# A hybrid encoder layer on one core: another way to the recurrence's decay, another order of the split products, and pools that wait by bytes

## The chip, the cores and the metric

The kernel runs on one core of one Trainium2 chip. The metric is the device time of one execution in microseconds (us), from the profiler's clock, as the median of several runs. The core has TensorE (PE, the matrix engine, with its weight loads listed as PEld), VectorE (DVE), ScalarE (ACT), GpSimd (POOL), and SyncE (SP), whose queue issues most of the DMA transfers.

## The reference, cut to what matters

One layer of a streaming encoder for 1,024 prompt tokens and 32 sample tokens, with 1,024 channels:

```python
z = x @ w_in + b_in                      # 12 sections of 1024 columns
# mixer A: short gated convolution; mixer C: HGRN2, a matrix state in 8 heads
# mixer B: a per-channel linear recurrence on the convolved section xf
r  = sigmoid(xf . w_a + b_a);  gi = sigmoid(xf . w_x + b_x)
log_a = -8 * r * softplus(-lam)
a  = exp(log_a)
u  = sqrt(-expm1(2 * log_a)) * (gi * xf)
h_t = a_t * h_{t-1} + u_t                # over the tokens
yB = (gelu(gB) * h) @ w_out_b
m  = sigmoid(gA)*yA + sigmoid(gB)*yB + sigmoid(gC)*yC
x  = LayerNorm(alpha*x + m @ w_o)
x  = LayerNorm(alpha*x + PEER(x))        # 8 heads x top 16 of 16,384 single-neuron experts
```

## The kernel before, in words

Channels lie on the 128 partitions and tokens along the free axis. The tokens go in two halves: half 0 is 512 prompt tokens, half 1 is the other 512 and the 32 sample tokens with a gap (548 columns, two segments of 274).

**Split products.** Every projection of the layer that decides which experts are chosen is done in three products: weight and activation are each split in a high and a low part. `weight` (line 286) loads a raw slice of 1024 x 128, casts it to `wh` on ScalarE (L292), and subtracts on VectorE to get `wl` (L293). Two buffers each of raw, `wh` and `wl` go round. `proj` (line 319) then walks over the 8 slices k of the contraction: `wh` times the activations' high part (L326), `wh` times their low part (L327), and `wl` times the high part (L329), for each of one or two segments, into PSUM tiles named `z`.

**Mixer B.** `mix_b` (line 555) does one tile of 128 channels: it is called 8 times for each half. After the gates' matmul (L585), ScalarE computes `tr` and `ti` (tanh forms of the two sigmoids, L589 and L591), `t` (L592, a tanh of half of -log_a) and `sq` (L593, the square root of t). VectorE computes 1/(1+t) (L599 or, in half 1, ScalarE's L597, then L600), a = 1 - 2t/(1+t) (L601, then L605 or, in half 1, ScalarE's L603), the input of the recurrence (L607 to L609), and the scan (L615).

**Stages and pools.** The SBUF is a stack of pools that stages open and close through `open` (line 118). A stage's pool often lies where an earlier stage's pool lay. Half 0's retrieval of experts (`topk`, `retrieve`) works in the pool `rp`, 12 buffers of 2,240 bytes a partition. It closes, and half 1's HGRN2 heads open `hp` (15,872 bytes) from the same start and `xe` (6 buffers of 2,208 bytes) behind it. `head_c` (line 627) evacuates its projection z of the query into an `xe` tile through ScalarE (L637), after two other `xe` tiles are made (L647, L648).

**Half 0's experts** are gathered token by token: GpSimd issues an indirect DMA for each of 1,024 rows of a table (L1210; four row buffers), and VectorE uses each row (L1219 for the table u, L1227 for v). These VectorE instructions are placed among the other VectorE work by counts of PE instructions (`pacing`). **Half 1's experts** are computed densely: `dense` (line 1103) walks over 16 chunks of 8 x 128 experts. In each, 8 hidden slices are projected (those of the first chunks are computed earlier), weighted (L1123) and split in `dh` and `dl` (L1127, L1128), and then 8 projections take these 8 pairs as their slices k.

**Order.** The program is traced in order, and a list scheduler with a timing model places each engine's instructions by priority and by when it thinks they are ready, so that an engine's order may differ from the trace's. On the chip, each engine then runs its list strictly in that order.

Of the kernel before, what the change touches and what calls it, by code (L numbers as in the profile page):

```python
# [16 lines left out]
AF = mybir.ActivationFunctionType  # L17
OP = mybir.AluOpType
# [4 lines left out]
KT = 8  # L23
# [48 lines left out]
FA = 2  # L72
# [29 lines left out]
class K:  # L102
# [15 lines left out]
    def open(self, ctx, **pools):  # L118

        for name, (bufs, kw) in pools.items():  # L120
            setattr(self, name, ctx.enter_context(self.tc.tile_pool(name=name, bufs=bufs, **kw)))

    def et(self, n=556, dt=F32):
        return self.ep.tile([128, n], dt, name="e", tag="e")
# [28 lines left out]
    def consts(self):  # L153
        nc, io, c = self.nc, self.io, self.cst
        V, A, G = nc.vector, nc.scalar, nc.gpsimd
# [28 lines left out]
        ct = ExitStack()  # L184
        t = ct.enter_context(self.tc.tile_pool(name="ct", bufs=1))
# [47 lines left out]
        e8 = lambda nm: c.tile([128, 8], F32, name=nm)  # L233
# [35 lines left out]
        self.sp2 = e8("sp2")  # L269
        V.tensor_scalar(u, u, 2.0, None, op0=OP.mult)  # L270
        V.scalar_tensor_tensor(self.sp2, p, 4.0, u, op0=OP.mult, op1=OP.add)


        self.ha = c.tile([128, 8, 2], F32, name="ha")
# [44 lines left out]
    def proj(self, w, x, lay):  # L319
        mm = self.nc.tensor.matmul  # L320
        z = self.zz(lay)
        wh, wl = w
        for k in range(KT):
            xh, xl = x[k]
            for (o, n), ps in zip(lay.segs, z):
                mm(ps[:, :n], wh[:, k, :], xh[:, o:o + n], start=k == 0, stop=False)  # L326
                mm(ps[:, :n], wh[:, k, :], xl[:, o:o + n], start=False, stop=False)  # L327
            for (o, n), ps in zip(lay.segs, z):
                mm(ps[:, :n], wl[:, k, :], xh[:, o:o + n], start=False, stop=k == KT - 1)  # L329
        return z  # L330
# [224 lines left out]
    def mix_b(self, ct, out):  # L555
        nc, par, b, L = self.nc, self.par, self.b, self.L
        V, A, mm, N = nc.vector, nc.scalar, nc.tensor.matmul, L.N
        col = lambda p: par[:, p + ct:p + ct + 1]
        zx = self.proj(self.win(B_X, ct), self.x, L)
        u = self.et()  # L560
        V.tensor_copy(u[:, 0:3], self.hbx[:, ct, :])
        for v, p in L.each(zx):
            A.activation(v(u, 3), p, AF.Identity, bias=col(B_X * 8))
        if b:
            V.tensor_copy(u[:, SO:SO + 3], par[:, P_SCB + 3 * ct:P_SCB + 3 * ct + 3])
            V.tensor_copy(self.st[:, 32 + 3 * ct:35 + 3 * ct], u[:, HB:HB + 3])
            V.tensor_copy(self.st[:, 56 + 3 * ct:59 + 3 * ct], u[:, SO + SMP:SO + SMP + 3])
        else:
            V.tensor_copy(self.hbx[:, ct, :], u[:, HB:HB + 3])
        cb = self.et()  # L570
        A.activation(cb[:, :N], u[:, 0:N], AF.Identity, scale=col(P_CBW), bias=col(P_CBB))
        for k in (1, 2, 3):
            V.scalar_tensor_tensor(cb[:, :N], u[:, k:k + N], col(P_CBW + 8 * k), cb[:, :N],
                                   op0=OP.mult, op1=OP.add)
        zg = self.proj(self.win(B_G, ct), self.x, L)
        g = self.et()
        for v, p in L.each(zg):
            A.activation(v(g), p, AF.Gelu, bias=col(B_G * 8))
        yield
        pr, pi = (self.zz(L), self.zz(L)) if b else ([self.tt()], [self.tt()])  # L580
        lw = self.lp.tile([128, 2, 128], F32, name="lw", tag="lw")
        nc.sync.dma_start(lw, self.io["lru_w"][ct])
        for j, z in enumerate((pr, pi)):
            for v, p in L.each(z):
                mm(p, lw[:, j, :], v(cb), start=True, stop=True)  # L585
        tr, ti, sq = self.et(), self.et(), self.et()
        t = tr
        for v, p in L.each(pr):
            A.activation(v(tr), p, AF.Tanh, scale=0.5, bias=self.hlb[:, ct:ct + 1])  # L589
        for v, p in L.each(pi):  # L590
            A.activation(v(ti), p, AF.Tanh, scale=0.5, bias=self.hlb[:, 8 + ct:9 + ct])  # L591
        A.activation(t[:, :N], tr[:, :N], AF.Tanh, scale=self.sp2[:, ct:ct + 1], bias=self.sp2[:, ct:ct + 1])  # L592
        A.activation(sq[:, :N], t[:, :N], AF.Sqrt)  # L593

        rc, a = self.et(), t
        if b and FA > 1:
            A.activation(rc[:, :N], t[:, :N], AF.Identity, bias=self.one)  # L597
        else:
            V.tensor_scalar(rc[:, :N], t[:, :N], 1.0, None, op0=OP.add)  # L599
        V.reciprocal(rc[:, :N], rc[:, :N])  # L600
        V.tensor_mul(a[:, :N], t[:, :N], rc[:, :N])  # L601
        if b and FA:
            A.activation(a[:, :N], a[:, :N], AF.Identity, scale=-2.0, bias=self.one)  # L603
        else:
            V.tensor_scalar(a[:, :N], a[:, :N], -2.0, 1.0, op0=OP.mult, op1=OP.add)  # L605
        v = ti
        V.scalar_tensor_tensor(v[:, :N], ti[:, :N], 1.0, cb[:, :N], op0=OP.add, op1=OP.mult)  # L607
        V.tensor_mul(v[:, :N], v[:, :N], sq[:, :N])
        V.tensor_mul(v[:, :N], v[:, :N], rc[:, :N])  # L609
        if b:  # L610

            V.memset(a[:, SO - 1:SO], 0.0)
            V.tensor_copy(v[:, SO - 1:SO], col(P_SLR))
        h = cb
        V.tensor_tensor_scan(h[:, :N], a[:, :N], v[:, :N], self.hl[:, ct:ct + 1],  # L615
                             op0=OP.mult, op1=OP.add)
        if b:
            V.tensor_copy(self.st[:, 80 + ct:81 + ct], h[:, HB - 1:HB])
            V.tensor_copy(self.st[:, 88 + ct:89 + ct], h[:, SO + SMP - 1:SO + SMP])
        else:  # L620
            V.tensor_copy(self.hl[:, ct:ct + 1], h[:, HB - 1:HB])
        r = self.yraw(True)
        V.tensor_mul(r[:, :N], g[:, :N], h[:, :N])
        out.append(self.yfin(r))
# [770 lines left out]
```

## Time and profile before

| | |
|---|---|
| median of 3 runs | 4206.25 us (4188.08 to 4211.31) |
| profiled execution, its own time | 4205.61 us |
| its span, first to last instruction | 4203.8 us |
| PE busy | 3815.1 us (91%), 26,917 matmuls |
| PE weight loads busy | 3564.2 us (85%) |
| VectorE busy | 3389.8 us (81%) |
| ScalarE busy | 1461.2 us (35%) |
| GpSimd busy | 1591.6 us (38%) |
| granted TensorE clock, mean | 0.952 of full speed |

The span and the profiled execution's own time differ by 1.8 us. Stages follow each other: up to about 740 us half 0's mixers, to about 1235 us half 0's norm and retrieval beside half 1's mixer A, to about 1670 us half 1's heads, to about 1970 us half 1's mixer B, to about 2340 us norm and retrieval, to about 2732 us the choice of experts spread to a dense form, and from there the dense experts. The gathers run from 988 us to the end.

### The profile page before, as it was taken

The page shows a single profiled execution, that of the slowest core. Times are in us where ns is not written, and L with a number is a line of the kernel's source. Part 1 is how long each engine was busy: PE and PEld are TensorE (multiplying, and loading weights), DVE is VectorE, ACT ScalarE, POOL GpSimd, SP SyncE. Part 2 cuts the span into 40 slices and gives each one's busy share as a digit, 9 for nine tenths or more (in the row PEclk, how much of TensorE's full clock was granted, in tenths as well). Part 3 has the DMA queues.
Part 4 walks back from the last instruction along what each step waited for, and adds up shares of the span by engine and source line. Part 5 has one row for each costly group of instructions (what it writes and reads, how often), then busy time and mean ns, then how long its engine had stood idle before and what let it go on. Part 6 is the DMA issues. An engine that isn't in the chain of part 4 may idle for free.

```text
span 4203.8 us, 69644 instructions
## 1 busy us (share of the span) xinstructions
PE 3815.1 (91%) x26917; PEld 3564.2 (85%) x26917; DVE 3389.8 (81%) x6793; ACT 1461.2 (35%) x2358; POOL 1591.6 (38%) x1353
## 2 busy tenths in 40 slices
PE   9999999998866998998878999789999999999997
PEld 7888777787765896998868999689999999999997
DVE  6565448589997787998899999967788878777888
ACT  3333337332212222454233389822222222222222
POOL 0000000002453344444552478823355555455553
PEclk9999999999887998999989999899999999999998
DMA  3222222345785666778986888698889988888886
GB/s 109 76 71 78 90 92 92 129 154 195 255 284 183 197 226 194 249 271 279 316 287 206 266 247 245 202 325 302 283 315 325 324 303 312 299 313 302 311 313 243
DMA packets 333451, 973.51 MB, mean 232 GB/s; under 512 B 29952, under 2 KB 104832, under 8 KB 331072
## 3 DMA queue, kind: packets, MB, share of 16 engines
q0 software_dynamic: 147456, 536.94, 37.6%
q1 hardware_dynamic: 185664, 432.12, 30.3%
q8 instruction: 212, 3.47, 0.3%
q14 instruction: 119, 0.97, 0.1%
HBM read 912.40 MB, written 56.54 MB: 230 GB/s over the span
## 4 chain that ended last, share of the span: by engine, by line
PE 50%; DVE 15%; issue 14%; DMA 10%; POOL 9%; ACT 2%; POOLq 0%; SPq 0%; DVEq 0%; ACTq 0%
PE z L329 14%; PE z L326 14%; PE z L327 14%; POOL row L1210 9%; DMA row<-in_v,ex 6%; DVE row L1219 2%; DVE wl L293 2%; DVE x1g L1227 2%; DMA row<-in_u,ex 2%; PE t L1073 2%; PE t L681 1%; PE z L336 1%; DVE oa L1069 1%; DVE e L960 1%; DVE e L959 1%
## 5 line engine op out<-in xcount | busy, mean ns | idle before, releaser
L326 PE MATMUL z<-h,wh 128*128 128x272 f32 (+5 forms) x4608 | 1381.8, 313 | 104.6 <-ACT xe L637 59.8
L327 PE MATMUL z<-l,wh 128*128 128x272 f32 (+5 forms) x4608 | 1377.5, 311 | 6.0 <-DVE l L908 4.8
L292 ACT CAST wh<-wraw 128x1024 fp32r<-128x1024 f32 x568 | 595.5, 1049 | 1850.5 <-PE z L327 1538.4
L1210 POOL DMA_INDIRECT row<-in_u,ex x512 | 669.0, 1307 | 1432.6 <-DVE ex L1033 667.5
L329 PE MATMUL z<-h,wl 128*128 128x272 f32 (+5 forms) x4608 | 1172.7, 312 | 10.2 <-DVE wl L293 10.1
L326 PEld LDWEIGHTS z<-h,wh 128*128 128x128 f32 x4608 | 883.0, 192 | 152.0 <-ACT xe L637 60.1
L1210 POOL DMA_INDIRECT row<-in_v,ex x512 | 682.9, 1334 | 797.5 <-DVE x1g L1227 532.2
L327 PEld LDWEIGHTS z<-l,wh 128*128 128x128 f32 x4608 | 883.4, 192 | 42.3 <-DVE l L908 5.9
L293 DVE TENSOR_TENSOR wl<-wraw,wh 128x1024 fp32r<-128x1024 f32 x568 | 692.4, 1220 | 232.5 <-ACT wh L292 231.2
L329 PEld LDWEIGHTS z<-h,wl 128*128 128x128 f32 x4608 | 778.3, 191 | 50.0 <-DVE wl L293 14.0
L1227 DVE SCALAR_TENSOR_TENSOR x1g<-row,hh,x1g 128x1024 f32<-128x1024 f32 x512 | 655.3, 1280 | 105.1 <-DMA row<-in_v,ex 101.6
L1219 DVE SCALAR_TENSOR_TENSOR row<-row,x1g 128x1024 f32<-128x1024 f32 x512 | 619.3, 1221 | 98.8 <-DMA row<-in_u,ex 98.0
L326 PE MATMUL z<-dh,wh 128*128 128x272 f32 x2048 | 556.2, 293 | 9.3 <-ACT ge L1084 4.9
L327 PE MATMUL z<-dl,wh 128*128 128x272 f32 x2048 | 558.2, 294 | 1.1 <-DVE dl L1128 1.1
L329 PE MATMUL z<-dh,wl 128*128 128x272 f32 x2048 | 436.0, 295 | 74.6 <-DVE wl L293 74.4
L326 PEld LDWEIGHTS z<-dh,wh 128*128 128x128 f32 x2048 | 391.5, 194 | 12.3 <-ACT ge L1084 5.2
L329 PEld LDWEIGHTS z<-dh,wl 128*128 128x128 f32 x2048 | 331.2, 194 | 79.4 <-DVE wl L293 79.4
L327 PEld LDWEIGHTS z<-dl,wh 128*128 128x128 f32 x2048 | 391.7, 193 | 1.7 <-DVE dl L1128 1.5
L1072 POOL TENSOR_SCALAR ob<-iota,tr 128x128 f32<-128x128 f32 x272 | 218.6, 818 | 29.4 <-PE t L1073 13.0
L329 PE MATMUL z<-yh,wl 128*128 128x512 f32 (+1 forms) x512 | 179.4, 353 | 22.5 <-DVE wl L293 22.4
L1127 ACT CAST dh<-w 128x544 fp32r<-128x544 f32 x128 | 82.5, 648 | 335.8 <-DVE w L1123 335.4
L1073 PE MATMUL t<-ob,oa 128*128 128x128 f32 x1088 | 172.8, 295 | 25.1 <-DVE oa L1069 8.5
(382 smaller groups left out, 4828.3 us busy)
## 6 DMA issues: line engine op xcount, KB each, us to landing
wraw<-in_w_in SPq DMA_DIRECT2D x192, 512.0 KB, 3.5
wraw<-in_vt SPq DMA_DIRECT2D x128, 512.0 KB, 6.4
wraw<-in_ut SPq DMA_DIRECT2D x128, 512.0 KB, 5.6
gd<-stg SPq DMA_DIRECT2D x34, 1024.0 KB, 6.1
gt<-gd SPq DMA_DIRECT2D x16, 2176.0 KB, 10.7
wraw<-in_wq SPq DMA_DIRECT2D x56, 512.0 KB, 4.3
wraw<-in_w_o SPq DMA_DIRECT2D x24, 512.0 KB, 4.9
hd<-ge SPq DMA_DIRECT2D x40, 272.0 KB, 4.8
```

What stands on the lines that cost most here:

```text
L292: nc.scalar.copy(wh, raw)
L293: nc.vector.tensor_sub(wl, raw, wh.bitcast(F32))
L326: mm(ps[:, :n], wh[:, k, :], xh[:, o:o + n], start=k == 0, stop=False)
L327: mm(ps[:, :n], wh[:, k, :], xl[:, o:o + n], start=False, stop=False)
L329: mm(ps[:, :n], wl[:, k, :], xh[:, o:o + n], start=False, stop=k == KT - 1)
L336: self.nc.tensor.matmul(ps[:, :n], w[:, k, :], x[k][:, o:o + n], start=k == 0, stop=k == KT - 1)
L1072: G.tensor_scalar(ob, self.iota, tr[:, 1, t:t + 1], None, op0=OP.is_equal)
L1073: nc.tensor.matmul(pw[:, s * 128:(s + 1) * 128], oa, ob, start=True, stop=True)
L1127: A.copy(hi, w)
L1210: nc.gpsimd.indirect_dma_start(out=u[:n], out_offset=None, in_=self.io[tab], in_offset=bass.IndirectOffsetOnAxis(ap=ex[:n, s:s + 1], axis=0))
L1219: V.scalar_tensor_tensor(u[:n], u[:n], 1.0, x1[:n], op0=OP.mult, op1=OP.mult, accum_out=hh[:n, s:s + 1])
L1227: V.scalar_tensor_tensor(x1[:n], u[:n], hh[:n, s:s + 1], x1[:n], op0=OP.mult, op1=OP.add)
```

## The change

It has three parts. In mixer B, `a` becomes an exponential on ScalarE with scale and bias `sp4` = -2 `sp2`; the reciprocal and the steps around it go; the recurrence's input becomes 0.5 (ti+1) cb (a+1) sq, which is the same quantity since 1/(1+t) = (1+a)/2. In `proj`, all products of the `wl` slices come behind all products of the `wh` slices. In `open`, each pool asks for waits by tile (`reuse_waits="tile"`): a tile waits for the earlier tiles whose bytes it takes, and no longer a whole pool for the whole of the earlier pools under it.

```diff
@@ def open
-            setattr(self, name, ctx.enter_context(self.tc.tile_pool(name=name, bufs=bufs, **kw)))
+            setattr(self, name, ctx.enter_context(self.tc.tile_pool(
+                name=name, bufs=bufs, reuse_waits="tile", **kw)))
@@ def consts
+        self.sp4 = e8("sp4")
+        V.tensor_scalar(self.sp4, self.sp2, -2.0, None, op0=OP.mult)
@@ def proj
                 mm(ps[:, :n], wh[:, k, :], xh[:, o:o + n], start=k == 0, stop=False)
                 mm(ps[:, :n], wh[:, k, :], xl[:, o:o + n], start=False, stop=False)
+        for k in range(KT):
+            xh, _ = x[k]
             for (o, n), ps in zip(lay.segs, z):
                 mm(ps[:, :n], wl[:, k, :], xh[:, o:o + n], start=False, stop=k == KT - 1)
@@ def mix_b
-        t = tr
+        t, a = sq, tr
...
         A.activation(t[:, :N], tr[:, :N], AF.Tanh, scale=self.sp2[:, ct:ct + 1], bias=self.sp2[:, ct:ct + 1])
+        A.activation(a[:, :N], tr[:, :N], AF.Exp, scale=self.sp4[:, ct:ct + 1], bias=self.sp4[:, ct:ct + 1])
         A.activation(sq[:, :N], t[:, :N], AF.Sqrt)
 
-        rc, a = self.et(), t
-        if b and FA > 1:
-            A.activation(rc[:, :N], t[:, :N], AF.Identity, bias=self.one)
-        else:
-            V.tensor_scalar(rc[:, :N], t[:, :N], 1.0, None, op0=OP.add)
-        V.reciprocal(rc[:, :N], rc[:, :N])
-        V.tensor_mul(a[:, :N], t[:, :N], rc[:, :N])
-        if b and FA:
-            A.activation(a[:, :N], a[:, :N], AF.Identity, scale=-2.0, bias=self.one)
-        else:
-            V.tensor_scalar(a[:, :N], a[:, :N], -2.0, 1.0, op0=OP.mult, op1=OP.add)
         v = ti
         V.scalar_tensor_tensor(v[:, :N], ti[:, :N], 1.0, cb[:, :N], op0=OP.add, op1=OP.mult)
-        V.tensor_mul(v[:, :N], v[:, :N], sq[:, :N])
-        V.tensor_mul(v[:, :N], v[:, :N], rc[:, :N])
+        V.scalar_tensor_tensor(sq[:, :N], a[:, :N], 1.0, sq[:, :N], op0=OP.add, op1=OP.mult)
+        V.scalar_tensor_tensor(v[:, :N], v[:, :N], 0.5, sq[:, :N], op0=OP.mult, op1=OP.mult)
```

## Rows read from the trace of the kernel before

**Rows 1.** Waits of all engines: who waited for whom, total us, times, longest

```profile
PE z L329 <- DVE wl L293: 113.7, 47, 11.0
...
PE z L326 <- ACT xe L637: 59.8, 2, 59.5
...
PE z L326 <- ACT wh L292: 46.0, 42, 9.2
```

**Rows 2.** Windows: length, busy us (count) by engine, clock, DMA share, GB/s

```profile
605.00:745.00 140.00, 140.00 (x578) 108.38 (x577) 113.65 (x141) 94.81 (x114) 0.00 (x0) 1.00 0.27 89
841.00:1261.00 420.00, 338.78 (x2497) 326.36 (x2496) 396.81 (x1304) 110.98 (x191) 133.36 (x105) 0.93 0.66 222
1727.00:1970.00 243.00, 223.76 (x1636) 218.31 (x1636) 228.44 (x343) 121.98 (x181) 108.83 (x80) 0.96 0.79 269
2732.00:4204.00 1472.00, 1357.68 (x10561) 1348.44 (x10559) 1182.54 (x1590) 374.58 (x552) 698.78 (x523) 0.96 0.86 305
3153.00:3363.00 210.00, 206.09 (x1640) 205.22 (x1639) 180.48 (x208) 56.84 (x88) 120.32 (x88) 1.00 0.91 325
```

**Rows 3.** Waits of PE alone from 2732 us to the end

```profile
PE z L329 <- DVE wl L293: 76.1, 22, 9.2
```

**Rows 4.** Timeline of PE: first and last of eight long waits in the dense stage

```profile
2834.29 0.82 PE L329 MATMUL z<-dh,wl 128*128 128x272 f32 x2 [9.13 <-DVE wl L293]
...
4038.37 0.52 PE L329 MATMUL z<-dh,wl 128*128 128x272 f32 x2 [3.87 <-DVE wl L293]
```

**Rows 5.** Timeline around 3510 us: PE, then VectorE

```profile
3514.26 0.82 PE L329 MATMUL z<-dh,wl 128*128 128x272 f32 x2 [6.47 <-DVE wl L293]
...
3511.40 1.28 DVE L1227 SCALAR_TENSOR_TENSOR x1g<-row,hh,x1g 128x1024 f32<-128x1024 f32 x1 [7.01 <-DMA row<-in_v,ex]
```

**Rows 6.** Window of 4 us behind that wait

```profile
3513.00:3517.00 4.00, 2.73 (x12) 2.74 (x13) 4.00 (x7) 0.00 (x0) 0.89 (x1) 0.50 0.74 243
```

**Rows 7.** Timeline from 1235 to 1296 us: PE, then ScalarE, then VectorE

```profile
1235.52 0.30 PE L329 MATMUL z<-h,wl 128*128 128x292 f32 x1
1295.36 0.58 PE L326 MATMUL z<-h,wh 128*128 128x256 f32 x1 [59.55 <-ACT xe L637]
...
1291.95 0.84 ACT L647 ACTIVATE xe<-e,f,f 128x544 f32<-128x544 f32 x1 [33.46 <-DVE ex L1033]
...
1291.56 0.29 DVE L1033 SCALAR_TENSOR_TENSOR ex<-r 128x128 int32<-128x128 f32 x1
```

**Rows 8.** Waits of SP's DMA queue

```profile
SPq L749 <- DVE ex L1033: 50.2, 1, 50.2
```

**Rows 9.** Mixer B by source line: count, then ns min/median/max

```profile
L592 ACT ACTIVATE e<-e,sp x16: 816/836/875, 619.7 to 1923.2; 128x512 f32<-128x512 f32 x8, 128x548 f32<-128x548 f32 x8
...
L593 ACT ACT_TABLE_LOAD  x16: 1283/1283/1283, 620.5 to 1927.6; - x16
...
L597 ACT ACTIVATE e<-e,one x8: 737/739/750, 1748.1 to 1931.3; 128x548 f32<-128x548 f32 x8
...
L599 DVE TENSOR_SCALAR e<-e x8: 420/427/428, 620.6 to 738.3; 128x512 f32<-128x512 f32 x8
...
L600 DVE RECIPROCAL e<-e x16: 3346/3440/3578, 621.0 to 1937.4; 128x512 f32<-128x512 f32 x8, 128x548 f32<-128x548 f32 x8
...
L601 DVE TENSOR_TENSOR e<-e x16: 679/700/730, 626.0 to 1948.6; 128x512 f32<-128x512 f32 x8, 128x548 f32<-128x548 f32 x8
```

**Rows 10.** Timeline, two chunk starts: first PE product, the last `dl` on VectorE

```profile
3809.79 0.29 PE L326 MATMUL z<-dh,wh 128*128 128x272 f32 x1
...
3820.82 0.72 DVE L1128 TENSOR_TENSOR dl<-w,dh 128x544 fp32r<-128x544 f32 x1
...
4021.78 0.29 PE L326 MATMUL z<-dh,wh 128*128 128x272 f32 x1
...
4025.84 0.72 DVE L1128 TENSOR_TENSOR dl<-w,dh 128x544 fp32r<-128x544 f32 x1
```

## The prediction

> **What bounds the kernel now.** I read the page first, then the waits, then windows by stage, and the timeline at the longest waits. PE is busy 3815.1 of 4203.8 us, so some 389 us of its idle time, and what the clock loses behind idle time, are all that a change which leaves the count of matmuls alone can win. The waits name the idle time [rows 1]: 113.7 us in 47 waits for the low weight part `wl`, one wait of 59.5 us for ScalarE's evacuation into an `xe` tile, and 46.0 us for the high part `wh`. By stage [rows 2] PE is full in half 0's mixer B (140.00 of 140.00 us), VectorE is nearly full from 841 to 1261 us (396.81 of 420), and the dense stage runs PE 1357.68 of 1472 us, with the DMA engines at 0.86. The window from 3153 us shows that stage undisturbed: 1640 matmuls in 210 us at full clock, 0.128 us each, DMA share 0.91.
>
> **The order of the products.** A projection of two segments is 48 matmuls. PE now meets `wl` after 4 of them; afterwards after 32, so `wl` may be 28 x 0.128 = 3.6 us later. (For one segment it is 14 matmuls, 1.8 us.) Nothing else is added: 48 products and as many weight loads stay. In the dense stage the 22 waits for `wl` sum to 76.1 us [rows 3]. Eight were longer than 3.6 us, from 9.13 down to 3.87 [rows 4], 52.1 us together; these keep 52.1 - 8 x 3.6 = 23.3 us, and the rest vanish, so 52.8 us would go. What makes `wl` late stays, though: at 3511 us VectorE stood 7.01 us at a gathered row and the subtraction was queued behind it [rows 5], and a faster PE asks for its weights sooner from DMA engines that have 0.86 to 0.91 of their time used. I take 45 us (bounds 25 and 53).
>
> The clock adds to this. After the 6.47 us wait it was granted 0.50, and PE did 12 matmuls in 2.73 busy us [rows 6] where 21 fit at 0.128: 9 x 0.128 = 1.2 us lost. Of the 16 dense waits of 1.8 us and more, the eight up to 3.6 us should end wholly: 8 x 1.2 = 10 us.
>
> The other 25 waits are 113.7 - 76.1 = 37.6 us. Most lie where VectorE leaves only 420 - 397 = 23 us [rows 2], and a wait taken off PE there partly comes back as a wait for VectorE's results. I take half, 18 us (bounds 5 and 30). `wh` is released after 32 matmuls of 48 instead of 46, 1.8 us earlier, so ScalarE can cast the next but one sooner; of the 46.0 us for `wh` most follow a late transfer, and I take 5 us (0 to 20).
>
> Against this, the last activations are needed earlier. A dense chunk's first projection starts while the eighth pair `dh`, `dl` is still being made. PE fills the time: it does 7 slices of the first projection and then 7 of the second, whose weights are the only others resident. That was 2 x 42 x 0.128 = 10.8 us of filler; afterwards the first pass of both gives 2 x 28 x 0.128 = 7.2 us, since their `wl` products stand behind the missing slice. The eighth `dl` came from 4.8 us (4021.78 to 4026.56) to 11.7 us (3809.79 to 3821.54) after the first product [rows 10]; in the eleven chunks from the sixth on, seven were later than 7.2 us, by 14 us together. Cost: 14 us (bounds 0 and 62, the second without any filler, below).
>
> **Pools that wait by bytes.** PE stopped at 1235.8 us with its PSUM tiles full, two of its projections waiting to be evacuated into `xe` tiles. ScalarE's first write to `xe` came at 1291.95, 0.1 us after VectorE's last instruction of half 0's retrieval (1291.56, 0.29 us long), and PE went on at 1295.36 [rows 7]: the whole pool waited for the whole pool. SP's queue stood 50.2 us at the same release, with the weights behind it [rows 8]. By bytes, `xe` begins 15,872 bytes into the old pool of 26,880 and ends at 29,120. Only its last buffer lies clear of retrieval tiles; the other five still wait for whichever tile of the last retrieval lies under them, the `hp` tiles do too, and ScalarE takes its list in order. So the gain lies between 0 and 59.5 us. I take a quarter, 15 us, nearer to nothing because one buffer in six is clear. The other stage changes show no wait of this kind that I can price; I take nothing for them.
>
> **The decay.** Each half-0 call drops on VectorE two scalar steps of 0.42, the reciprocal 3.44 and a product 0.70 us, 5.0 us; each half-1 call drops 3.44 + 0.70 = 4.1 us [rows 9]. Two products of the input become two of another form, taken as equal. Eight calls of each make VectorE 40 and 33 us lighter. ScalarE gains an exponential like L592 (0.84 us) and, if it needs a table of its own between the tanh's and the square root's, one more load of 1.28 us: 2.1 us a call, less 2 x 0.74 us for L597 and L603 in half 1. In half 0 all of it is hidden: PE is busy 140.00 of 140.00 us, and ScalarE goes from 94.81 to 112 us [rows 2]; without that cover it would be 8 x 2.1 = 17 us. In half 1 PE idles 243 - 223.76 = 19 us; most of that is for weights, counted above, and I take 3 us (-17 to 10).
>
> The Trainium skill (ScalarE: Activation LUTs, Table sets: the hidden batching unit) speaks against this part: it has the exponential and the square root in different sets, so that one behind the other means a load each. The trace has the load at 1.28 us; the page's own budget of about 2.66 us for a switch would make it an estimated 16 x (2.66 + 0.84) = 56 us of ScalarE's time in place of 34. By the same page tanh lies in the exponential's set too, so some loads may fall to a neighbour. No row here shows an exponential between the two.
>
> **The sum.** 45 + 10 + 18 + 5 + 15 + 3 - 14 = 82 us. From the profiled execution's 4205.61 us that gives 4124 us. Its own time is 0.6 us under the median of the runs, 4206.25, so nothing is corrected for that. The runs shown spread by 0.5%, about what a measurement of this kernel can tell from no change, 21 us.
>
> **The rivals.**
>
> *The long wait goes whole.* If the scheduler places the query's evacuation early and gives it a clear buffer, 59.5 us go instead of 15: 4124 - 45 = 4079 us. For it speaks that two evacuations free four of six PSUM tiles; against it the bytes and SP's queue.
>
> *The waits for `wl` only move.* VectorE's lateness comes from gathered rows, and those from DMA engines at 0.86 and more [rows 2, 5]. If the DMA sets the pace, PE's waits return elsewhere, and of the dense 55 us and the other 18 us a quarter and a half stay: 4124 + 41 + 9 = 4174 us. Against it speaks the window from 3153 us, with full clock at 0.91.
>
> *The table loads reach the path.* If the square root's result, late by 2.1 us in each of 16 calls, holds up PE, the time is 4124 + 34 = 4158 us. Against it speaks that VectorE's chain in the same call gets over 4 us shorter.
>
> *Slower: PE waits for the last `dl`.* If the scheduler finds no filler, PE stops 3.7 us after the first product (29 x 0.128) until the eighth `dl`, which comes at 8.1 us at the median: 4.4 us and 1.2 us of clock in each of eleven chunks, 62 us. This is then the same lateness under another name, so the dense 55 us don't come either: 4205.6 - (18 + 5 + 15 + 3) + 62 = 4227 us. It decides from 41 / 11 = 3.7 us a chunk on. Against it: PE's lists already hold such filler.
>
> **How the numbers follow.** The forecast has a chance of 0.50, with a range of its own from 4085 to 4165 us (its bounds taken together by halves). The whole wait has 0.17, the moved waits 0.17, the table loads 0.08, the slower case 0.08. From 4045 (the whole wait with the terms at their upper bounds) to 4195 us (the moved waits with some chunk waits) about 0.8 is held. Faster than 4185 are the forecast and the whole wait, most of the tables' case and three quarters of the moved one less a little for terms that all fall short: 0.82. Slower than 4227 is half of the last rival and what I can't see: 0.06. Within: 0.12.
>
> **What the profile afterwards would show.** Right: PE's waits for `wl` near 50 us in all, in the dense stage some ten in place of 22; mean clock above 0.952; no reciprocal in mixer B and VectorE's total about 73 us lower; 16 loads more on ScalarE at most; PE going on after 1235 us some 15 us earlier. Wrong: long PE waits for `dl` at chunk starts; waits for `wl` as many and as long as before; a new wait at an exponential; or the 59.5 us wait unchanged or gone.

## The result and the profile after

The changed kernel takes 4139.89 us (median of 4 runs, 4132.19 to 4149.73), the kernel before beside it on the same chip 4202.66 (4 runs). The ratio is 0.9855 [0.982, 0.9891]: faster by 62.8 us, where 82 were forecast. The profiled execution took 4132.19 us with a span of 4130.4, 73.4 us shorter than that of before; it is the shortest of the four runs, and the landmarks below are its own.

The busy time per engine on the page of the changed kernel:

```profile
PE 3792.2 (92%) x26917; PEld 3553.3 (86%) x26917; DVE 3320.1 (80%) x6746; ACT 1490.5 (36%) x2367; POOL 1578.8 (38%) x1353
```

The count of matmuls is unchanged; VectorE is 69.7 us lighter (3389.8 before). The mean granted clock rose from 0.952 to 0.958. TensorE's waits over the whole span (total us, times, longest), to be held against [rows 1]:

```profile
PE z L329 <- ACT xe L632: 60.1, 1, 60.1
PE z L329 <- ACT wh L295: 39.4, 16, 6.0
PE z L334 <- DVE wl L296: 36.3, 18, 4.1
```

The waits for `wl` fell from 113.7 to 36.3 us, those for `wh` by 6.6, and the one long wait for `xe` is as long as it was. From 2700 us to the end, against [rows 3]:

```profile
PE z L334 <- DVE wl L296: 25.3, 8, 4.1
PE z L330 <- DVE dl L1123: 18.6, 16, 2.7
PE z L329 <- ACT dh L1122: 7.4, 12, 1.2
```

Here the waits for `wl` lost 50.8 us. But `dl` and `dh`, for which TensorE had waited 2.4 us in this stage, now cost 26.0 us: nearly half of what the new order took away came back under two other names. Most of it lies in the first five chunks, whose hidden slices were computed earlier. TensorE's waits from 2711 to 3000 us, in which these chunks fall:

```profile
PE z L330 <- DVE dl L1123: 15.2, 11, 2.7
PE z L329 <- ACT dh L1122: 5.6, 8, 1.2
```

In the kernel before the same chunks (2754 to 3050 us) had waits of 25.0 us for `wl` and 2.4 for the pair. So there the new order wins little; from the sixth chunk on the waits for `wl` fell from 51.1 to 25.3 us, and the pair costs 5.3. Windows (length, busy us and count by engine, clock, DMA share, GB/s), beside [rows 2]: three of the changed kernel, of which the second is the stretch in which TensorE stands at `xe` and the third the dense stage, and last the dense stage of the kernel before, from its first product:

```profile
605.00:745.00 140.00, 140.00 (x578) 108.31 (x577) 80.06 (x112) 103.78 (x123) 0.00 (x0) 1.00 0.30 95
...
1209.00:1285.00 76.00, 9.05 (x49) 8.29 (x49) 70.67 (x184) 7.78 (x15) 43.20 (x38) 0.58 0.82 268
...
2711.00:4130.00 1419.00, 1335.94 (x10408) 1325.42 (x10408) 1178.78 (x1587) 375.32 (x547) 688.98 (x522) 0.97 0.88 312
...
2756.00:4204.00 1448.00, 1338.62 (x10408) 1329.61 (x10408) 1173.55 (x1580) 368.40 (x539) 696.67 (x521) 0.96 0.86 304
```

Half 0's mixer B leaves TensorE full, as before, with VectorE at 80.06 us in place of 113.65. The dense stage, from its first product to the end of the span, went from 1447.8 to 1418.8 us.

The long wait, in the timeline (start, duration, engine, instruction, idle time before it and what ended it), TensorE first, then ScalarE, then VectorE, against [rows 7]:

```profile
1208.28 1.24 PE L334 MATMUL z<-h,wl 128*128 128x292 f32 x8
1269.66 0.58 PE L329 MATMUL z<-h,wh 128*128 128x256 f32 x1 [60.14 <-ACT xe L632]
...
1240.32 0.31 ACT L988 ACTIVATE r<-r 128x128 f32<-128x128 f32 x1 [30.79 <-DVE r L987]
1266.25 0.84 ACT L642 ACTIVATE xe<-e,f,f 128x544 f32<-128x544 f32 x1 [25.62 <-DVE r L1022]
...
1265.54 0.67 DVE L1022 TENSOR_REDUCE r<-r 128x64 f32<-128x512 bf16 x1
1284.92 0.29 DVE L1028 SCALAR_TENSOR_TENSOR ex<-r 128x128 int32<-128x128 f32 x1
```

The waits by bytes work: ScalarE writes `xe` at 1266.25 us, after a reduce of the retrieval and 18.7 us before the retrieval's last instruction, where before it was 0.1 us behind that. TensorE goes on 25.7 us earlier than before. It also came to the stop 26 us earlier, so the wait keeps its length.

ScalarE's table loads at the exponential (L598) and the square root (L599), and the instruction of VectorE behind them, with the idle time of its engine before it, over all 16 calls:

```profile
L599 ACT ACT_TABLE_LOAD x16 | 20.5, 1283 | 0.1
L598 ACT ACT_TABLE_LOAD x13 | 16.7, 1283 | 0.2
...
L603 DVE SCALAR_TENSOR_TENSOR e<-e 128x512 f32<-128x512 f32 (+1 forms) x16 | 11.3, 707 | 33.0 <-ACT e L599 33.0
```

The exponential needs a load in 13 of 16 calls and the square root one in each, at 1.28 us a load. The Trainium skill has the two functions in different sets (ScalarE: Activation LUTs, Table sets: the hidden batching unit), and the trace agrees: the root, right behind the exponential, needs its load in every call. The page's 2.66 us for a switch (What ACT_TABLE_LOAD costs) holds a drain beside a load of this size; this trace shows only 0.3 us of idle time before the 29 loads. In the whole program there are 70 in place of 61. What the forecast did not look at is in the last column: VectorE now stands 33.0 us for ScalarE's square root, time that the reciprocal used to fill; 30.5 of them are in half 0, where TensorE stays full.

### The profile page after: what moved, and what is told of

Read it like the earlier page. It is cut to its first block, busy times and chain, and to the rows that moved or that the text cites. A ratio compares the mean times of both kernels' runs of the same rounds, so it can differ in the third digit from the quotient of the medians.

```text
span 4130.4 us, 69554 instructions
## 1 busy us (share of the span) xinstructions
PE 3792.2 (92%) x26917; PEld 3553.3 (86%) x26917; DVE 3320.1 (80%) x6746; ACT 1490.5 (36%) x2367; POOL 1578.8 (38%) x1353
## 4 chain that ended last, share of the span: by engine, by line
PE 27%; DMA 11%; issue 11%; DVE 9%; POOL 8%; ACT 1%; POOLq 0%; DVEq 0%; SPq 0%; ACTq 0%
PE z L334 8%; POOL row L1205 8%; PE z L329 7%; PE z L330 7%; DMA row<-in_v,ex 7%; DMA row<-in_u,ex 3%; DVE x1g L1222 2%; DVE oa L1064 2%; PE t L1068 1%; DVE wl L296 1%; PE z L341 1%; DVE row L1214 1%; DMA wraw<-in_w_in 1%; PE t L676 1%; DMA ge<-hd 0%
## 5 line engine op out<-in xcount | busy, mean ns | idle before, releaser
L329 PE MATMUL z<-h,wh 128*128 128x272 f32 (+5 forms) x4608 | 1324.4, 314 | 105.5 <-ACT xe L632 60.1
L330 PE MATMUL z<-l,wh 128*128 128x272 f32 (+5 forms) x4608 | 1315.7, 312 | 3.0 <-DVE l L903 1.9
L1205 POOL DMA_INDIRECT row<-in_u,ex x512 | 652.7, 1275 | 1393.7 <-DVE ex L1028 667.8
L334 PE MATMUL z<-h,wl 128*128 128x272 f32 (+5 forms) x4608 | 745.1, 309 | 3.7 <-DVE wl L296 3.7
L334 PEld LDWEIGHTS z<-h,wl 128*128 128x128 f32 x4608 | 649.2, 189 | 37.9 <-DVE wl L296 4.7
L330 PE MATMUL z<-dl,wh 128*128 128x272 f32 x2048 | 518.2, 293 | 18.9 <-DVE dl L1123 18.6
L329 PE MATMUL z<-dh,wh 128*128 128x272 f32 x2048 | 513.6, 293 | 8.5 <-ACT dh L1122 7.4
L334 PE MATMUL z<-dh,wl 128*128 128x272 f32 x2048 | 286.1, 293 | 25.3 <-DVE wl L296 25.3
L334 PEld LDWEIGHTS z<-dh,wl 128*128 128x128 f32 x2048 | 271.9, 193 | 27.1 <-DVE wl L296 27.1
L329 PE MATMUL z<-yh,wh 128*128 128x512 f32 (+1 forms) x512 | 171.4, 352 | 19.8 <-ACT wh L295 19.8
```

Source lines behind the costliest of these rows:

```text
L1205: nc.gpsimd.indirect_dma_start(out=u[:n], out_offset=None, in_=self.io[tab], in_offset=bass.IndirectOffsetOnAxis(ap=ex[:n, s:s + 1], axis=0))
```

## The experiments

The change has three parts, so the first runs take them apart. Times are medians, each against the runs of the kernel before on its chip (4199.8 to 4209.1 us).

**Each part alone, and one pair.** The four kernels are the kernel before with a part of the diff each:

```
order:   proj() in two passes over k, wl last
pools:   tile_pool(name=name, bufs=bufs, reuse_waits="tile", **kw)
decay:   mix_b with Exp, without reciprocal
```

*Order alone.* 

> Only the order of the products is changed. Theory (each part gives what its term says, and the order carries the change): about 45 us faster than before, near the 63 us of the whole change less the pools and the decay; dense stage about 29 us shorter, its waits for wl near 25 us with new waits for dl and dh near 26 us; the 59.5 us wait for the xe tile stays and ends at VectorE's last instruction of the retrieval. Rival (the pools free the later stages): 30 us or less faster, with the norm and top-k stage between the mixers and the dense experts as long as before.

*Pools alone.* 

> Only the pools' waits are changed. Theory: the release of the first xe tile comes some 19 us ahead of the last instruction of the retrieval, PE goes on that much earlier, the heads give some of it back: 8 to 15 us faster, waits for wl as before (about 114 us). Rival (pools decide more stages): 30 us or more faster, with the norm and top-k stage some 20 us shorter. Second rival: no difference, since the heads give all of it back.

*Decay alone.* 

> Only the recurrence's decay is changed. Theory: within 5 us of before; VectorE's busy time about 73 us lower, 9 more table loads on ScalarE, nothing of either on the path, as PE is full in half 0's mixer B and has 19 us idle in half 1's. Rival (table loads on the path): 10 to 30 us slower. Second rival (VectorE was the bound of half 1's mixer B): 10 us or more faster.

*Order and decay.* 

> The whole change without the pools' part. Theory (parts add): 50 us faster than before, 13 us short of the whole change; the wait for the xe tile ends at the retrieval's last instruction again. Rival (the pools' gain is given back by the heads): the same as the whole change, about 63 us faster.

Order alone: 4170.53 us, ratio 0.9933 [0.991, 0.9955], 29 us faster. Pools alone: 4196.78, 0.9989 [0.9976, 1.0002], no difference that can be told. Decay alone: 4184.76, 0.9966 [0.995, 0.9982], 15 us. Order and decay: 4152.21, 0.9891 [0.9868, 0.9914], 48 us.

Held against what was expected: the order alone has the rival's time (30 us or less), though its dense stage did what the theory says of the waits (26.4 us for `wl`, 25.6 for the pair) and the stage between mixers and dense experts got shorter too, which the rival excluded. The pools alone are the second rival: no difference. The decay alone is beyond the theory's 5 us and fits the second rival, in which VectorE was the bound of half 1's mixer B. Order and decay fit the theory, 48 us for 50.

The order does not bring what its waits lose. TensorE's waits in the kernel with the order alone:

```profile
PE z L326 <- ACT xe L639: 73.7, 1, 73.7
PE z L326 <- ACT wh L292: 36.7, 15, 5.9
PE z L331 <- DVE wl L293: 35.3, 16, 4.3
```

The waits for `wl` fell by 78 us, while the wait for `xe` grew from 59.5 to 73.7 us: what TensorE wins in front of half 1's heads, it stands off there, because VectorE's retrieval ends when it did (1285.5 against 1291.6 us). With order and decay that wait is 80.2 us; the pools bring it to 60.1. With the order alone it is 73.7, with the pools too 54.7. So beside the new order the pools take 19 to 20 us off it. Without the new order they take less: 59.5 falls to 52.6 us, and with the decay 63.5 to 51.5.

**Two parts of three.** The same pieces, the decay left out, then the order left out.

> The kernel before with the new order of the slices and with the pools' waits by bytes, without the exponential. Order alone gave -29 us, pools alone nothing that can be measured, order and decay together -48, the whole change -63: the pools are worth some 14 us in company. Theory: they pay where the order has already taken away the waits for low slices, so this kernel is 43 us faster than before (ratio near 0.990) and its long wait of TensorE for a tile of xe ends at about 1274 us of the span. Rival: they pay only with VectorE's freed time (the retrieval's reduces, which now release xe, come earlier by the decay): then this kernel is -29 to -32 us (ratio near 0.993).

> The changed kernel with the old order of the slices: decay and pools alone. Known: order alone -29 us, pools alone -3 (nothing that can be measured), decay alone -15, order and pools -37, order and decay -48, all three -62. The three alone give 47, so some 15 us come only in company. Theory: they come where the order meets the other two, so that without it decay and pools give what they give alone: -18 us, ratio near 0.9957. Rival: they come where the decay meets the pools (the reduces that hold the bytes of xe come earlier on a lighter VectorE): then this kernel is -33 us, ratio near 0.992.

Order and pools: 4164.78 us, 0.9906 [0.9882, 0.993], 37 us. Decay and pools: 4183.27, 0.9949 [0.9937, 0.9961], 22 us. The second speaks for the theory (18 us) and against a meeting of decay and pools (33). The first lies between its two numbers, and its long wait ends at 1265.5 us, where the theory had 1274. With the kernel before and the whole change these six make all eight combinations, so each part can be read four times, from nothing else changed to both others changed: order 29, 33, 34 and 40 us, decay 15, 18, 19 and 26, pools 3, 7, 8 and 15. Alone they sum to 47 us, and together they give 63. The whole change is known to some 15 us either way and the others to 5 to 10, so this excess of 16 us is not settled; the wait for `xe` above is a mechanism for it that the traces show.

**The reciprocals put back, beside the exponential.** In the kernel with the decay alone:

```
 A.activation(sq[:, :N], t[:, :N], AF.Sqrt)
+rc = self.et()
+V.tensor_scalar(rc[:, :N], t[:, :N], 1.0, None, op0=OP.add)
+V.reciprocal(rc[:, :N], rc[:, :N])
```

> The exponential alone, as in the run of the decay alone, but VectorE still computes tanh + 1 and its reciprocal in each of the 16 channels, into a tile that nothing reads: 16 x (427 + 3440) ns = 62 us of VectorE's time are put back, the result is the reference's. Theory: the decay's 15 us come from VectorE's freed time, so they go, and the time is within 5 us of the kernel before. Rival: they come from ScalarE's side (the decay is there earlier, the extra passes of half 1 are gone): the kernel stays 10 to 15 us faster than before.

4224.81 us, 1.0054 [1.0037, 1.0071]: neither number. It is 23 us slower than the kernel before, where the decay alone is 15 us faster, though VectorE's 3379.8 us are fewer than before. The edit was harsher than meant: the square root is written in place over the tanh, so the added pair reads the root and stands behind it. VectorE's timeline of this kernel, in the first call:

```profile
624.06 0.43 DVE L599 TENSOR_SCALAR e<-e 128x512 f32<-128x512 f32 x1 [4.07 <-ACT e L596]
624.52 3.35 DVE L600 RECIPROCAL e<-e 128x512 f32<-128x512 f32 x1
627.79 0.63 DVE L604 SCALAR_TENSOR_TENSOR e<-e 128x512 f32<-128x512 f32 x1
628.34 1.21 DVE L295 TENSOR_TENSOR wl<-wraw,wh 128x1024 fp32r<-128x1024 f32 x1
```

VectorE first stands 4.07 us for ScalarE, then takes 3.35 for the reciprocal, and only then makes `wl`. TensorE, full in this window in the kernel before, is busy 131.82 of 140 us:

```profile
605.00:745.00 140.00, 131.82 (x533) 99.30 (x532) 94.08 (x113) 101.74 (x119) 0.00 (x0) 1.00 0.24 81
```

In the kernel before the same `wl` is made 3.5 us earlier, since there the reciprocal doesn't wait for the root:

```profile
621.02 3.35 DVE L600 RECIPROCAL e<-e 128x512 f32<-128x512 f32 x1
...
624.83 1.21 DVE L293 TENSOR_TENSOR wl<-wraw,wh 128x1024 fp32r<-128x1024 f32 x1
```

So a reciprocal behind the root is not free there; whether one that reads the tanh would be, as was meant, this run doesn't tell. VectorE is less busy here than before (94.08 against 113.65 us, beside 533 matmuls for 578), and yet late, by the place of its work and not by its sum.

**Half 1's first heads kept off `xe`.** On the changed kernel:

```
-P, kk = self.xt(), self.xt()
+xt = self.et if b and h < 2 else self.xt
+P, kk = xt(), xt()
...
-q = self.xt()
+q = xt()
```

> The changed kernel, but in half 1 the first two heads take their tiles P, kk and q from the tiles at the right end of SBUF and not from xe, whose bytes the retrieval's tiles still hold. Theory: TensorE's wait of 60 us at 1209.5 is for those bytes (ScalarE can't empty PSUM into them), so TensorE goes on for at least two heads' products, the wait shrinks by 25 us or more, and the time falls to 4095 to 4115 us. Rival: VectorE, which is with the retrieval until 1285 us, can't take up the heads any earlier, so TensorE stops a little later for the next thing (a tile of the heads, or a low weight slice that VectorE makes), waits as much in sum, and the time stays within 5 us of the changed kernel.

4141.17 us, 0.985 [0.982, 0.988], as the changed kernel (4139.89). The rival holds. The wait for `xe` is gone and another stands in its place, ended by the same retrieval, in TensorE's and ScalarE's timeline:

```profile
1285.64 2.07 PE L677 MATMUL t<-e 128*128 128x128 f32 x8 [68.16 <-ACT vs L657]
...
1285.00 0.59 ACT L657 COPY vs<-t 128x512 f32<-128x512 f32 x1 [38.46 <-DVE r L1022]
```

`vs` is a tile of `hp`, whose bytes the retrieval's tiles hold too. Which pool waits is not what matters; the end of the retrieval on VectorE is.

**What VectorE does meanwhile.** From 1209 to 1285 us it is busy 70.67 of 76 us. The largest groups of the changed kernel in that window are not the retrieval's:

```profile
L1214 DVE SCALAR_TENSOR_TENSOR row<-row,x1g 128x1024 f32<-128x1024 f32 x38 | 46.1, 1222 | 6.2 <-DMA row<-in_u,ex 6.2
L1205 POOL DMA_INDIRECT row<-in_u,ex x38 | 44.5, 1170 | 33.1 <-DVE row L1214 16.9 <-issue 3.0 <-DVE gw L1030 2.5
L1022 DVE TENSOR_REDUCE r<-r 128x64 f32<-128x512 bf16 (+1 forms) x6 | 5.7, 946 | 0.0
```

Thirty-eight dots of the first half's experts take 46.1 us, and each has a read of its accumulator of 81 ns behind it. Two runs move 50 such dots out of the way, by the list of how many go beside each stage:

```
BESIDE = 92, 125, 145, 94, 42, 82, 444   # changed kernel
BESIDE = 42, 140, 155, 104, 47, 92, 444  # dots later
BESIDE = 42, 125, 145, 94, 42, 82, 494   # dots into dense
```

> The changed kernel with another schedule of VectorE's work for the first half's experts: in the stage that ends at TensorE's wait of 60 us it issues 42 dots with gathered rows in place of 92, the other 50 are spread over the four stages behind it (140, 155, 104, 47 and 92 in place of 125, 145, 94, 42 and 82); nothing is left out. VectorE is busy 70.7 of the 76 us from 1209 to 1285, 49.2 of them with 38 such dots, which stand between the pieces of the retrieval that holds the bytes of xe. Theory: VectorE's list holds the retrieval and with it TensorE, so the retrieval ends 40 to 60 us earlier, the wait falls to 20 us or less and the time to 4105 to 4125 us, some of the 40 us being given back where the 50 dots go. Rival: the stages behind are as full on VectorE (0.81 of the heads, 0.92 of the mixers, 0.91 of the second retrieval), and the 65 us of dots hold TensorE there: within 5 us of the changed kernel.

> As the run with the dots later, but all 50 dots go into the dense stage (494 in place of 444), the other stages keep theirs. Theory (VectorE is spare there: busy 1179 of 1419 us): the wait before the heads falls to 20 us or less, the stages between lose nothing, the dense stage grows by less than 15 us, and the time is 4100 to 4115 us, under that of the run with the dots spread. Rival: the low slices of the dense stage's weights and the pair dh, dl stand behind each dot on VectorE, so its waits for wl and dl grow by the 65 us that the dots take, and nothing is won against the changed kernel.

Dots later: 4175.1 us, 0.9932 [0.9914, 0.995], 35 us slower than the changed kernel by the medians. Dots into dense: 4203.96, 0.9989 [0.9977, 1.0001], 64 us slower. In both the wait for `xe` falls to 15 us and the retrieval ends some 60 us earlier (1223.4 and 1226.2 us), which is what the theory says of it; the heads end 31.5 and 27 us earlier. Then it is all given back, and more. Dots later loses it in the second retrieval: the stretch from the heads' end to the end of the last product with the keys is 665.6 us in place of 629.5. The same 377 matmuls of it in the changed kernel and in this one:

```profile
2073.90:2154.70 80.80, 55.23 (x377) 51.63 (x376) 76.53 (x121) 29.43 (x68) 46.97 (x26) 0.82 0.82 279
```

```profile
2053.40:2163.40 110.00, 61.10 (x377) 54.92 (x376) 92.97 (x169) 27.33 (x64) 62.35 (x41) 0.73 0.83 285
```

They take 110.0 us in place of 80.8, beside 42 rows in place of 26, and TensorE waits 31.1 us in place of 9.9 for the low parts that VectorE makes of the normed tokens (`l`, L903). Dots into dense has lost its lead at the last product with the keys too (2279.7 against 2279.1 us), though the stages up to there kept their dots, against the theory; why, no run here shows. It is 16 us ahead again at the first dense product (2695.8 against 2711.6 us), level at TensorE's last (4097.5 against 4099.1), and loses its time behind that. Its dense stage, and what follows it:

```profile
2696.00:4098.00 1402.00, 1343.05 (x10408) 1332.15 (x10406) 1152.14 (x1535) 363.24 (x527) 694.93 (x526) 0.98 0.88 314
4098.00:4211.00 113.00, 0.00 (x0) 0.00 (x0) 85.43 (x101) 9.04 (x16) 62.02 (x46) 0.51 0.75 252
```

The rows went no faster for being more: from 3100 to 4100 us this kernel does 396 of them and the changed one 399, and 49 more follow from 4100 to 4202. Neither the theory (a dense stage under 15 us longer) nor the rival (65 us more of waits for `wl` and `dl`) had this. The 60 us wait is the price of dots that neither of the two other places takes without a greater loss.

**The low part last at a chunk's start.** On the changed kernel, for d == 0 of the dense chunks:

```
 for k: for segments: mm(wh, xh);  if not late: mm(wh, xl)
 for k: for segments: mm(wl, xh)
+if late: for k: for segments: mm(wh, xl)
```

> The changed kernel, but in the first of the eight projections of a dense chunk the products with the activations' low part dl come last, behind those with the weights' low slice. Theory: the 18.6 us in 16 waits for dl at the chunks' starts are a price of the new order, as forecast (14 us), and this takes them away: the waits for dl fall under 3 us, and the time falls by 10 to 18 us. Rival: the weights' low slice, which is now wanted earlier in that projection, or the next chunk's dh, is late in its place: the waits only change their name, and the time stays within 5 us.

4149.54 us, 0.9875 [0.9846, 0.9903]: 10 us over the changed kernel by the medians, which the intervals don't tell apart from no difference, and no gain. TensorE's waits from 2650 us on:

```profile
PE z L329 <- ACT dh L1127: 26.1, 22, 4.5
PE z L331 <- DVE dl L1128: 18.0, 12, 3.2
PE z L335 <- DVE wl L296: 17.7, 8, 3.5
```

In time the rival holds, but this is no full test of the theory. The edit reaches one projection of each chunk, and TensorE fills its waits with the next one, which still wants `dl` early. The groups of matmuls that read `dl`, those of the seven other projections (L331) and the late ones of the edit (L339), each with its busy time, the mean ns of one, and TensorE's idle time before it:

```profile
L331 PE MATMUL z<-dl,wh 128*128 128x272 f32 x1792 | 460.4, 292 | 18.0 <-DVE dl L1128 18.0
...
L339 PE MATMUL z<-dl,wh 128*128 128x272 f32 x256 | 34.7, 288 | 0.0
```

Where `dl` is wanted late, TensorE waits for it no more. All 18.0 us stand at projections that the edit left alone, in the first five chunks. From the sixth on the waits for `dl` are gone (3.5 us before), those for `wl` are 7.6 us shorter, and those for `dh` 14.5 us longer (16.3 for 1.8): there the wait did move to another part of the pair. What `dl` last in both projections would give was not tried.

**Without the last tile's rows.** On the changed kernel:

```
-for s in range(128):
+for s in range(ns):   # 4 for the last tile, 128 for the others
```

> The changed kernel without most of the experts' work of the last of the four tiles: 8 of its 256 gathered rows, with their dots and sums on VectorE, are kept, 248 are left out; its part of the output is not the reference's. The dense stage keeps some 190 rows, all in its first part; about the last 800 us have hardly any. From 3300 to 4080 us of the changed kernel TensorE waits 28.5 us: 23.2 in 7 waits for wl, 3.5 for dl, 1.8 for dh. Theory: what is left of the waits of the dense stage comes from VectorE standing at late rows with the subtractions behind it, so without rows the waits in the last 780 us before the last chunk's end fall under 5 us together, and the kernel is 20 to 45 us faster than the changed one (the tail after the last product grows shorter too). Rival: the weights' transfers are what is late (DMA share 0.90 there): the waits stay at 15 us or more, under wl or wh.

4107.6 us, 0.9758 [0.9734, 0.9783]: 32 us faster than the changed kernel by the medians, 41 by the ratios. The rows end at 3495 us. From 3300 to 4080 TensorE still waits 13.0 us, more than the theory's 5, but all of it before 3500, while rows still run; after that there is no wait at all, where the changed kernel has 19.1 us. The same 560 us in the changed kernel and in this one:

```profile
3520.00:4080.00 560.00, 540.81 (x4252) 538.37 (x4250) 463.08 (x598) 146.81 (x222) 308.37 (x224) 0.99 0.90 318
```

```profile
3520.00:4080.00 560.00, 560.00 (x4474) 559.95 (x4473) 214.08 (x288) 158.18 (x231) 0.00 (x0) 1.00 0.32 109
```

With no rows TensorE is busy 560.00 of 560.00 us. The weights come in time by themselves; the rows, through VectorE's list or the DMA engines that they share with the weights (share 0.90 with rows, 0.32 without), are what the waits in this part come from. Which of the two it is, this run doesn't part, since it takes both away. Of the waits for the pair in the first five chunks it says nothing: the rows there were kept, and the waits too (19.5 us for 20.8).

## Why the prediction was right, and where its sizes were not

The forecast was 4124 us, the median is 4139.89: inside the forecast's own range, and 62.8 us of gain for 82. By its own steps:

- **Dense waits for `wl` (45 us):** right in sum. They lost 50.8 us, eight stay where ten were forecast, and 25.3 us where 23.3 were worked out from the long ones [rows 4] (the longest of these was 9.2 us; 9.13 is the first). That the sums agree so closely is luck: by the same working 7.6 us were to stay in the first five chunks, where none stays, and 15.7 from the sixth on, where 25.3 stay.
- **The clock behind them (10 us):** mostly missing in this stage. A lower clock lengthens TensorE's busy time [rows 6], and for the same 10,408 matmuls that fell by only 2.7 us (1338.62 to 1335.94), at a mean clock of 0.97 in place of 0.96; the waits for `wl`, `dl` and `dh` together fell by 27.2 of the stage's 29.0 us. Over the whole span the busy time fell by 22.9 us for the same matmuls, so some 20 us of that lie ahead of the dense stage, where the step priced nothing.
- **The last `dl` (14 us against):** under-sized, and looked for in the wrong chunks. The waits for the pair are 26.0 us, 23.6 more than before, in 28 waits, and 7.4 us of them are for `dh`, which the step left out. It counted the eleven chunks from the sixth on [rows 10], and there the pair costs 5.3 us. The other 20.8 are in the first five chunks, which it did not count. By the kernel's text, no hidden projections stand between the pairs there; that this is why they come late was not tested.
- **Other waits for `wl` (18 us of 37.6):** the waits fell further, to 11.0 us, but half of such a gain comes back, as assumed: with the order alone 14.2 us of it stand again in the wait for `xe`. Order alone gives 29 us, in company 33 to 40, where its terms sum to 45 + 10 + 18 + 5 - 14 = 64. This is where most of the missing gain is.
- **`wh` (5 us):** 6.6 us less wait.
- **Pools (15 us):** the size is right with both other parts (15 us), and not alone (3, by the ratio 5 [-1, 10]) or with one of them (7 and 8). The step had the wait end 15 us earlier; it ends 9 us earlier with the pools alone and 20 us earlier when they join order and decay. Its reasoning on the bytes held: the writer is released by a reduce and not by the last instruction. The rival in which the wait goes whole failed for a reason that the forecast didn't name: 46 us of experts' dots in the retrieval's way.
- **Decay (3 us, -17 to 10):** the mis-sized term on the other side, beyond its upper bound: 15 us alone [8, 21], up to 26 in company. The cover in half 0 was right: TensorE is busy 140.00 of 140.00 us there with it. What failed is the step that priced half 1's mixer B by TensorE's idle time and put that down to weights. VectorE was the bound there. From 1762 to 1930 us, the kernel before and the decay alone:

```profile
1762.00:1930.00 168.00, 159.85 (x1171) 155.48 (x1169) 165.00 (x253) 89.07 (x131) 77.60 (x58) 0.98 0.78 264
```

```profile
1762.00:1930.00 168.00, 165.13 (x1238) 160.75 (x1237) 156.91 (x274) 98.91 (x138) 90.73 (x68) 1.00 0.87 303
```

VectorE was busy 165.00 of 168 us; with the decay TensorE does 67 more matmuls in the same time. From the heads' end to the last scan of mixer B on VectorE the kernel before takes 294.0 us and the decay alone 281.4. In the other pairs of kernels the decay shortens this by 10.6 us (beside the pools), 2.6 (order) and 8.0 (both). What it gives behind the mixers is not parted so well: from the heads' end to the end of the last product with the keys the decay alone takes 635.6 us in place of 657.4, but order alone has 637.5 and the pools alone 649.7.

- **The table loads on the path (rival):** no. There are 70 loads in place of 61, VectorE stands 33.0 us for the root, and half 0's TensorE stays full. With a reciprocal behind the root it does reach the path (23 us slower than before, where the decay alone is 15 faster).
- **Slower by waits for `dl` (rival):** the waits came (26.0 us), at under half of its 62: the longest is 2.7 us, where it had 4.4 in each of the chunks from the sixth on, and in these the waits are 5.3 us in all.

The span before the dense stage gained 44.4 us in the profiled runs, against 18 + 5 + 15 + 3 = 41 forecast; the dense stage 29.0 against 45 + 10 - 14 = 41. The near agreement of the first hides errors of both signs. Of the 44.4 us, 28 lie between the heads' end and the last product with the keys, for which the forecast had the decay's 3 us and a share of the 18. That stretch, before and after, with 4084 matmuls in each:

```profile
1664.09:2321.53 657.44, 569.69 (x4084) 549.00 (x4084) 602.81 (x1214) 249.23 (x407) 288.46 (x218) 0.92 0.78 264
```

```profile
1649.59:2279.11 629.52, 557.07 (x4084) 540.82 (x4084) 570.80 (x1197) 256.69 (x406) 297.58 (x216) 0.94 0.80 275
```

VectorE, at 0.92 of this stretch the busiest engine before, is 32 us lighter; TensorE's idle time fell by 15 us and its busy time by 13, at a clock of 0.94 in place of 0.92.

## What to carry to other kernels

A wait that a reordering takes off the fullest engine is worth only what the next late operand leaves: price the order's new first-needed operand everywhere the order applies, also where nobody waited for it before, and look for the next place where the engine stops for the same producer. When a long wait is for a pool, look at what the producer does during the wait before touching the pool: here two thirds of it was background work, which cost more in the later stages it was moved to. An engine's sum of busy time over the whole kernel says little by itself. What taking work off it is worth is read where it is full (165.00 of 168 us here), and the same work placed behind another engine's result made TensorE wait, with VectorE less busy than before.

## What the runs showed of the hardware that was not expected

- The gathered rows kept a pace that more of them did not raise: 399 in 1000 us of the dense stage with 444 placed there, 396 with 494, at a DMA share of 0.89 to 0.90: 2.5 us a row. The others ran on behind the last product, where the weight stream is over and the DMA share 0.75, and 49 of them still took 102 us, 2.1 us a row. What sets this pace was not separated: the transfers, the round trip through four row buffers, or in the dense stage the order of VectorE's list.
- A tanh behind a Gelu needed no table load: in the changed kernel the 16 calls of mixer B had loads at the Gelu (14), the exponential (13) and the square root (16), and none at the tanh that follows the Gelu (L594). So three of 16 exponentials found their table already there.
- VectorE less busy can be later: 94.08 us of 140 with TensorE short of `wl`, where 113.65 us had kept it full.
